# A decoder trunk on one core: embeddings loaded earlier and multiplied by eights, plain columns kept in banks, transposes by eights, longer runs of token-major pieces

## The chip, the cores and the metric

The kernel runs on one core of a Trainium2 chip. The metric is the device time of one execution in microseconds (us). TensorE (PE) multiplies, VectorE (DVE) and ScalarE (ACT) do elementwise work, GpSimd (POOL) and SyncE (SP) issue DMAs here. PE writes its products to PSUM, eight banks of 512 float32 columns on 128 partitions.

## The reference, cut to what matters

Two layers on 256 tokens of 2048 features: a gated linear-attention layer, then a forgetting-attention layer. Each ends with an MLP and a gated per-layer embedding, and these two are what the change touches:

```python
D_MODEL = 2048; SEQ = 256; DEPTH = 2; PLE_DIM = 256; D_FF = 4 * D_MODEL

def sq_relu_mlp(u, w_up, w_down):
    hid = jax.nn.relu(u @ w_up)
    return (hid * hid) @ w_down

for layer in range(DEPTH):
    u = rms_norm(h, mix_norm[layer])
    ...
    h = h + sq_relu_mlp(rms_norm(h, mlp_norm[layer]), w_mlp_up[layer], w_mlp_down[layer])
    gate = jax.nn.sigmoid(rms_norm(h, ple_norm[layer]) @ w_ple_gate[layer])
    h = h + (p[layer] @ w_ple_up[layer]) * gate
    ...
return rms_norm(h, final_norm)
```

All is float32. `p` is the embedding, 256 features for each token and layer.

## The kernel before

Activations lie feature-major: features on partitions, the 256 tokens along the row. Every float32 matrix is split into a rounded part `hi` and a rest `lo` (`split`, L105 to L111: ACT makes `whi` in L108, DVE makes `wlo` in L109), and a product is three matmuls: hi times hi, hi times lo, lo times hi. Weights come by the SP queue as tiles `raw` of 1 MB in three buffers; each tile is split in two halves of 1024 columns, for which there are four buffers `whi` and four `wlo`. What is normed by a row factor is multiplied first and scaled after (`rstd`).

A feature-major product (`mm_split`, L120 to L129) holds weights in PE and streams 256 tokens: 48 matmuls of 256 columns (L126 to L128) for one tile `ps` of 128 features. A token-major one (`product`, L292 to L299) holds activations and streams 512 weight columns: 12 matmuls for one piece.

The MLP (`mlp`, L239) goes through the 8192 hidden features in eight blocks of 1024. `up(b, i)` makes one tile of 128 hidden features: 48 matmuls, relu and scaling on DVE (L275), square on ACT (L277), split (`plain_split`, L219 and L220); for tiles 4 to 7 also four differences of it (L287), split in L289 and L290. The down product of a block is made while the next block's up tiles are made. Half of its columns go through seven products p1 to p7 on sums of quarters of the weights, in place of eight plain ones: the sums come into a buffer `chain` by DMAs that add, from the POOL queue (L258). The other half, the plain columns, goes through four pieces n0 to n3 of 24 matmuls. A finished product lies in a bank `pp` (four of them; the tiles `ps` have the other four) and is added to an accumulator in SBUF (`into`, L301 to L307). The order in which the pieces are written stands in a string of names in L390; the framework's scheduler may still move single instructions on an engine.

Behind the last block stands the last stage (L396 to L421): the accumulators are combined (L398); `h`, put away in DRAM at the start since `chain` has its place, is loaded again by POOL (L401); the eighth block's hidden tiles are multiplied feature-major, 24 matmuls for each of 16 tiles (L412 to L414), and with each tile go two transposes (L417) that bring the token-major sums back. Two adds to `h` follow (L418, L419), then the next layer's input is scaled and split (`u_p`) and its squares are summed (`ssq`).

Then the gate (`ple`, L424) opens a pool of its own, loads the embeddings by POOL (`praw`, L431), splits them to `pt` (L434), and for each of 16 tiles makes six matmuls of `pt`, which ACT copies to SBUF (L442), and 48 of `u_p`, scaled by `rstd`, put through a sigmoid (L449), multiplied and added to `h` (L453, L454). In layer 0 each column is then scaled and split twice for the next layer.

Of the kernel before, what the change touches and what calls it, by code (L numbers as in the profile page):

```python
# [10 lines left out]
F32 = mybir.dt.float32  # L11
# [7 lines left out]
P = 128  # L19
T = 256  # L20
D = 2048
KC = D // P
NBL = 8
NH = 16
# [10 lines left out]
def yoco_kernel(ctx, tc, a, out):  # L35
# [84 lines left out]
    def mm_split(pairs, act, kcs=KC, off=0):  # L120
        ps = psm.tile([P, T], F32, name="ps", tag="mm")
# [110 lines left out]
    def mlp(layer, u, stats, slots, u2, g2, pool, pps):  # L232
# [26 lines left out]
        acc = {}  # L259
        st2 = Stats()  # L260

        def up(b, i):
# [22 lines left out]
            x = pool.tile([P, 4, P], F32, name="sums", tag="sums", bufs=1)  # L285
# [23 lines left out]
        def bank():  # L309
            return pps.tile([P, 512], F32, name="pp", tag="pp", bufs=4)  # L310
# [11 lines left out]
        def down(b):  # L322
# [9 lines left out]
            got = {}  # L332
# [66 lines left out]
        sums = [(acc["2"], acc["4"]), (acc["3"], acc["7"]), (acc["n00"], acc["n01"]), (acc["n10"], acc["n11"])]  # L399
# [3 lines left out]
        last = a["w_down"][layer, 3 * KC :, :, 1024:].rearrange("n p f -> p n f")  # L403
        for n in range(KC):
# [4 lines left out]
            ps = psm.tile([P, T], F32, name="ps", tag="mm")  # L409
            for k in range(8):  # L410
                wh, wl = (w[:, k * P : (k + 1) * P] for w in pairs[n % 2])
                nc.tensor.matmul(ps, wh, nf[:, k, 0, :], start=k == 0, stop=False)  # L412
                nc.tensor.matmul(ps, wh, nf[:, k, 1, :], start=False, stop=False)  # L413
                nc.tensor.matmul(ps, wl, nf[:, k, 0, :], start=False, stop=k == 7)  # L414
# [560 lines left out]
```

## Time and profile before

| what | value |
|---|---|
| median of three runs | 2463.29 us (2462.58 to 2463.54) |
| the profiled execution, its span | 2462.49 us, 2460.8 us |
| PE, DVE, ACT, POOL busy in the span | 99%, 73%, 57%, 5% |
| granted TensorE clock, mean | 0.995 |
| matmuls recorded | 18024 |

The span is from the first to the last instruction; 1.7 us lie around it. Matmuls are pipelined, so one of 256 columns is recorded with 0.28 us although they start 0.11 apart; the distance between starts is what one costs in a run. The granted clock is 1.00 at 2.4 GHz and 0.50 at 1.2 GHz. Rows of the timeline have the start from the span's beginning, the duration, the engine, the line, out<-in, and in brackets how long the engine sat idle before and what ended it.

### The profile page before, as it was taken

The numbers are of one execution on the slowest core, as the hardware profiler recorded it, in microseconds if no ns is written. First come the engines' busy times: TensorE is split into PE (matmuls) and PEld (weight loads), VectorE is DVE, ScalarE is ACT, GpSimd is POOL, SyncE is SP. The second block draws the span as 40 slices with busy tenths as digits, with TensorE's granted clock in tenths as the row PEclk, the third lists the DMA queues.
The fourth block names the chain that finished last, engine by engine and source line by source line (L and its number), as shares of the span: only waits on it lengthen the run. The fifth ranks groups of instructions, "written<-read, shape, count | busy, mean of one in ns | idle before, by whom it ended". The sixth has DMA issues, their size and how long they took to land.

```text
span 2460.8 us, 43678 instructions
## 1 busy us (share of the span) xinstructions
PE 2437.6 (99%) x18024; PEld 2315.2 (94%) x18024; DVE 1801.9 (73%) x2802; ACT 1406.2 (57%) x2128; POOL 119.0 (5%) x159
## 2 busy tenths in 40 slices
PE   9999999999999999999999999999999999999998
PEld 8999999999999999999999999999999999999998
DVE  7897797676777777778774566667677777777866
ACT  7666575566555555555654545556655555555554
POOL 1000000000000000000000000000000000000000
PEclk9999999999999999999999999999999999999999
DMA  6455455578877887785555655557887888778653
GB/s 248 172 185 186 174 179 197 212 251 240 238 224 241 242 233 231 230 232 216 175 179 189 198 171 178 174 210 263 234 236 227 235 244 228 236 233 224 221 174 122
DMA packets 129271, 521.73 MB, mean 212 GB/s; under 512 B 8688, under 2 KB 9264, under 8 KB 91696
## 3 DMA queue, kind: packets, MB, share of 16 engines
q1 hardware_dynamic: 88256, 415.66, 47.4%
q0 software_dynamic: 39520, 101.25, 19.2%
q8 instruction: 141, 2.31, 0.4%
q10 hardware_dynamic: 1296, 2.03, 0.2%
q14 instruction: 58, 0.48, 0.1%
HBM read 512.58 MB, written 6.32 MB: 211 GB/s over the span
## 4 chain that ended last, share of the span: by engine, by line
PE 99%; DMA 0%; DVE 0%; ACT 0%; issue 0%; ACTq 0%; DVEq 0%; POOLq 0%
PE ps L126 21%; PE ps L127 21%; PE ps L128 21%; PE pp L297 8%; PE pp L299 8%; PE pp L298 8%; PE pst L146 2%; PE pst L145 2%; PE pst L147 2%; PE ps L412 1%; PE ps L414 1%; PE ps L413 1%; PE pa L635 0%; PE pl L837 0%; PE ptr L417 0%; DMA praw<-in_pT 0%
## 5 line engine op out<-in xcount | busy, mean ns | idle before, releaser
L109 DVE TENSOR_TENSOR wlo<-raw,whi 128x1024 fp32r<-128x1024 f32 (+2 forms) x798 | 965.7, 1211 | 420.8 <-ACT whi L108 411.4
L108 ACT CAST whi<-raw 128x1024 fp32r<-128x1024 f32 (+2 forms) x798 | 830.7, 1042 | 768.4 <-PE ps L127 585.4
L127 PE MATMUL ps<-u_m,whi 128*128 128x256 f32 x2048 | 565.2, 276 | 0.0
L126 PE MATMUL ps<-u_m,whi 128*128 128x256 f32 x2048 | 565.2, 276 | 0.0
L128 PE MATMUL ps<-u_m,wlo 128*128 128x256 f32 x2048 | 565.0, 276 | 0.0
L126 PEld LDWEIGHTS ps<-u_m,whi 128*128 128x128 f32 x2048 | 384.4, 188 | 4.3
L127 PEld LDWEIGHTS ps<-u_m,whi 128*128 128x128 f32 x2048 | 384.4, 188 | 4.3
L128 PEld LDWEIGHTS ps<-u_m,wlo 128*128 128x128 f32 x2048 | 384.6, 188 | 0.0
L298 PE MATMUL pp<-wlo,hid 128*128 128x512 f32 x840 | 327.3, 390 | 0.0
L299 PE MATMUL pp<-whi,hid 128*128 128x512 f32 x840 | 327.3, 390 | 0.0
L297 PE MATMUL pp<-whi,hid 128*128 128x512 f32 x840 | 318.6, 390 | 0.0
L108 ACT CAST whi<-chain 128x1024 fp32r<-128x1024 f32 x168 | 176.6, 1051 | 130.7 <-PE pp L299 78.0
L109 DVE TENSOR_TENSOR wlo<-chain,whi 128x1024 fp32r<-128x1024 f32 x168 | 204.7, 1223 | 51.7 <-ACT whi L108 48.6
L126 PE MATMUL ps<-u_a,whi 128*128 128x256 f32 x768 | 213.9, 279 | 0.0
L128 PE MATMUL ps<-u_a,wlo 128*128 128x256 f32 x768 | 213.2, 278 | 0.0
L127 PE MATMUL ps<-u_a,whi 128*128 128x256 f32 x768 | 212.3, 276 | 0.0
L299 PEld LDWEIGHTS pp<-whi,hid 128*128 128x128 f32 x840 | 157.7, 188 | 33.6
L298 PEld LDWEIGHTS pp<-wlo,hid 128*128 128x128 f32 x840 | 157.7, 188 | 29.1
L297 PEld LDWEIGHTS pp<-whi,hid 128*128 128x128 f32 x840 | 157.6, 188 | 29.0
L258 POOL DMA_DIRECT2D chain<-in_w_down x84 | 93.4, 1112 | 1104.9 <-DVE wlo L109 856.9
L126 PEld LDWEIGHTS ps<-u_a,whi 128*128 128x128 f32 x768 | 144.3, 188 | 0.3
L127 PEld LDWEIGHTS ps<-u_a,whi 128*128 128x128 f32 x768 | 144.3, 188 | 0.2
(289 smaller groups left out, 4704.1 us busy)
## 6 DMA issues: line engine op xcount, KB each, us to landing
raw<-in_w_up SPq DMA_DIRECT2D x128, 1024.0 KB, 6.1
raw<-in_w_down SPq DMA_DIRECT2D x86, 1024.0 KB, 5.2
chain<-in_w_down POOLq DMA_DIRECT2D x84, 1024.0 KB, 8.3
raw<-in_w_ain SPq DMA_DIRECT2D x48, 1024.0 KB, 4.8
raw<-in_w_pg SPq DMA_DIRECT2D x32, 1024.0 KB, 4.8
raw<-in_w_vf SPq DMA_DIRECT2D x20, 832.0 KB, 4.3
raw<-in_w_aout SPq DMA_DIRECT2D x16, 1024.0 KB, 4.8
raw<-in_w_k SPq DMA_DIRECT2D x16, 1024.0 KB, 4.7
```

Of the source, the lines that this page charges most:

```text
L108: nc.scalar.copy(h_, r)
L109: nc.vector.tensor_tensor(l_, r, h_.bitcast(F32), op=ALU.subtract)
L126: nc.tensor.matmul(ps, wk(pair, kl, 0), act[:, k, 0, :], start=st, stop=False)
L127: nc.tensor.matmul(ps, wk(pair, kl, 0), act[:, k, 1, :], start=False, stop=False)
L128: nc.tensor.matmul(ps, wk(pair, kl, 1), act[:, k, 0, :], start=False, stop=sp)
L145: nc.tensor.matmul(o, act[:, kk, 0, tok], hi, start=st, stop=False)
L146: nc.tensor.matmul(o, act[:, kk, 0, tok], lo, start=False, stop=False)
L147: nc.tensor.matmul(o, act[:, kk, 1, tok], hi, start=False, stop=sp)
L258: eng.dma_start(dst.rearrange("p (n f) -> p n f", n=4), src, **kw)
L297: nc.tensor.matmul(o, xh, hi, start=start and j == 0, stop=False)
L298: nc.tensor.matmul(o, xh, lo, start=False, stop=False)
L299: nc.tensor.matmul(o, xl, hi, start=False, stop=stop and j == 3)
```

## The change

Six things, in both layers:

- `embeddings` (L442 of the changed kernel on) loads `praw` and makes `pt` in the MLP's pool, called before the last stage. `praw` takes the place of the squares of the hidden tiles (`sqrs`), `pt` that of `scr`, in which relu results and sums lay.
- The gate multiplies `pt` by eights: before tiles 0 and 8, 48 matmuls for eight tiles go into four banks, two tiles to a bank, and ACT copies each bank in one go to accumulators that are free by then.
- The plain columns stay in four banks `pn00` to `pn11` over the seven blocks and are copied once, by ACT, to `nsum`. The products p1 to p7 share the four banks of the tiles `ps`.
- The transposes are made eight at a time (`back`), into two banks, and DVE adds two tiles of `h` at once.
- The string of the order has two up tiles in a row and then two to three token-major pieces.
- The gate lies inside the MLP's pools.

```diff
-    def mm_split(pairs, act, kcs=KC, off=0):
-        ps = psm.tile([P, T], F32, name="ps", tag="mm")
+    def mm_split(pairs, act, kcs=KC, off=0, ps=None):
+        if ps is None:
+            ps = psm.tile([P, T], F32, name="ps", tag="mm")
...
+        scr = pool.tile([P, 4 * T + 64], F32, name="scr", tag="scr", bufs=1)
+        squares = pool.tile([P, 3, T], F32, name="sqrs", tag="sqrs", bufs=1)
+        turn = [0, 0]
+
+        def part(which):
+            i = turn[which]
+            turn[which] = (i + 1) % (2 + which)
+            return squares[:, i, :] if which else scr[:, i * T : (i + 1) * T]
...
-            t = pool.tile([P, T], F32, name="up", tag="up", bufs=2)
+            t = part(0)
...
-            s = pool.tile([P, T], F32, name="hsq", tag="hsq", bufs=3)
+            s = part(1)
...
-        def bank():
-            return pps.tile([P, 512], F32, name="pp", tag="pp", bufs=4)
+        nbank = [[pps.tile([P, 512], F32, name=f"pn{c}{t}", tag=f"pn{c}{t}") for t in range(2)] for c in range(2)]
...
             def one(name, op, pairs):
-                o = bank()
+                o = psm.tile([P, 512], F32, name="pp", tag="mm")
...
-                if q == 0:
-                    got[c] = [bank() for _ in range(2)]
                 for t in range(2):
-                    product(got[c][t], lambda j: tuple(nf[:, 4 * q + j, w, t * P : (t + 1) * P] for w in range(2)), pairs, q == 0, q == 1)
-                if q == 1:
-                    for t in range(2):
-                        into(f"n{c}{t}", got[c][t])
+                    product(nbank[c][t], plain(q, t), pairs, b == q == 0, b == NBL - 2 and q == 1)
...
-            for item in "up p1 up p2 n0 up p5 up p3 n1 up p6 up n2 p7 up p4 up n3".split():
+            for item in "up up p1 p2 n0 up up p5 p3 n1 up up p6 n2 p7 up up p4 n3".split():
...
+        pt = embeddings(layer, pool)
...
+        nsum = pool.tile([P, 4, 512], F32, name="nsum", tag="nsum", bufs=1)
+        for i in range(4):
+            nc.scalar.copy(nsum[:, i], nbank[i // 2][i % 2])
...
+        def back(m):
+
+            for i in range(2):
+                n = 4 * m + 2 * i
+                ptr = pps.tile([P, 2, T], F32, name="ptr", tag=f"pn{m % 2}{i}")
+                for j in range(2):
+                    for t in range(2):
+                        nc.tensor.transpose(ptr[:, j, t * P : (t + 1) * P], sums[m][t][:, (n + j) % 4 * P : ((n + j) % 4 + 1) * P], ident)
+                nc.vector.tensor_tensor(h[:, n : n + 2, :], ptr, h[:, n : n + 2, :], op=ALU.add)
...
+            ps = mm_split([pairs[n % 2]], nf, 8)
+            if n % 4 == 0:
+                back(n // 4)
             nc.vector.tensor_tensor(h[:, n, :], ps, h[:, n, :], op=ALU.add)
-            nc.vector.tensor_tensor(h[:, n, :], pt, h[:, n, :], op=ALU.add)
...
+    def embeddings(layer, pool):
+        praw = pool.tile([P, 3, T], F32, name="praw", tag="sqrs", bufs=1)[:, :2, :]
+        pt = shifted(pool, 2, "pt", "scr", PTS)
         nc.gpsimd.dma_start(praw, a["pT"][layer])
         for k in range(2):
             plain_split(pt, k, praw[:, k, :])
+        return pt
...
-            pu = mm_split(wu, pt, kcs=2, off=2 * (n % 8))
-            up = pool.tile([P, T], F32, name="up", tag="up", bufs=2)
-            nc.scalar.copy(up, pu)
+                for i in range(4):
+                    pu = pps.tile([P, 2, T], F32, name="pu", tag=f"pn{i // 2}{i % 2}")
+                    for j in range(2):
+                        mm_split(wu, pt, 2, 4 * i + 2 * j, pu[:, j, :])
+                    nc.scalar.copy(ups[i], pu)
```

What this makes of the order on PE is shown at three places. The first is the end of the last stage of layer 0, before (`ptr` are the transposes, `accn` accumulators of the plain columns, `pt` the embeddings, `u_p` the gate's input):

```order
L412 MATMUL ps<-hid_7_11857,whi 128x256
L413 MATMUL ps<-hid_7_11857,whi 128x256
L414 MATMUL ps<-hid_7_11857,wlo 128x256
L417 MATMUL ptr<-ident,accn_7578 128x128
L417 MATMUL ptr<-ident,accn_7580 128x128
L126 MATMUL ps<-pt,whi 128x256
L126 MATMUL ps<-u_p_12733,whi 128x256
```

and now, on PE at the same place:

```order
L128 MATMUL ps<-hid_7_11671,whi 128x256
L129 MATMUL ps<-hid_7_11671,whi 128x256
L130 MATMUL ps<-hid_7_11671,wlo 128x256
L128 MATMUL pu<-pt,whi 128x256
L129 MATMUL pu<-pt,whi 128x256
L130 MATMUL pu<-pt,wlo 128x256
```

The transposes that stood behind the sixteenth tile have moved up to the thirteenth, and the embeddings' matmuls follow the tile's own; 48 of them stand there before the first of `u_p`.

The second place is PE in the middle of n0 of the first block now (`pn` are the banks of the plain columns, `ps` is the next up tile):

```order
L309 MATMUL pn_6164<-whi,hid_0_6168 128x512
L309 MATMUL pn_6165<-whi,hid_0_6168 128x512
L128 MATMUL ps<-u_m_5112,whi 128x256
L129 MATMUL ps<-u_m_5112,whi 128x256
L310 MATMUL pn_6164<-wlo,hid_0_6168 128x512
L311 MATMUL pn_6164<-whi,hid_0_6168 128x512
```

Two matmuls of the next up tile have moved in between the first two of n0's second half and the rest of it. It is so in n0 and in n1 of each of the 14 blocks, 28 times; before, a piece held none.

The third is the POOL queue around the reload of `h`, now (with the semaphores that each row waits for):

```order
L260 DMA chain<-in_w_down 128x4x512 [waits DMASW7_49,DVE_49]
L260 DMA chain<-in_w_down 128x4x512 [waits DMASW2_49,DVE_49]
L410 DMA h<-res 128x4096 [waits DMASW4_49,DMASW3_49,DVE_49]
L440 DMA praw<-in_pT 128x512 [waits DVE_49,PE_49,Pool_49]
L796 MEMSET cmask 128x128 [waits DVE_49,DMASW6_49,PE_49,Activation_49]
```

The DMAs stand in the order they had; what `praw` waits for on VectorE is now the split of the last hidden tile, and its wait for PE is for work of the attention before the MLP, where it was the last transpose of the stage.

## Rows read from the trace of the kernel before

**Rows 1.** The page: span, busy time of the engines, the granted clock of TensorE in 40 slices (tenths), and the chain that ended last by engine.

```profile
span 2460.8 us, 43678 instructions
PE 2437.6 (99%) x18024; PEld 2315.2 (94%) x18024; DVE 1801.9 (73%) x2802; ACT 1406.2 (57%) x2128; POOL 119.0 (5%) x159
...
PEclk9999999999999999999999999999999999999999
...
PE 99%; DMA 0%; DVE 0%; ACT 0%; issue 0%; ACTq 0%; DVEq 0%; POOLq 0%
```

**Rows 2.** The two largest of the waits of PE: who waited, for whom, us in total, times, the longest.

```profile
PE ps L126 <- ACT pt L219: 8.2, 2, 4.1
PE pst L145 <- ACT whi L108: 2.2, 1, 2.2
```

**Rows 3.** Timeline of all engines at the end of layer 0's MLP.

```profile
1168.76 0.38 PE L417 MATMUL ptr<-ident,accn 128*128 128x128 f32 x2
...
1169.71 0.57 POOL L431 DMA_DIRECT2D praw<-in_pT  x1 [64.11 <-DVE h L418]
...
1171.06 0.48 DVE L216 SCALAR_TENSOR_TENSOR u_p<-h,gains,u_p 128x256 fp32r<-128x256 f32 x1
...
1172.75 0.71 ACT L219 CAST pt<-praw 128x256 fp32r<-128x256 f32 x2 [1.99 <-DMA praw<-in_pT]
...
1173.21 0.58 PE L126 MATMUL ps<-pt,whi 128*128 128x256 f32 x1 [4.07 <-ACT pt L219]
```

**Rows 4.** DMA issues with the median time from issue to landing (line, queue, times, KB each, us), and from the timeline of POOL the issue of the reload.

```profile
h<-res POOLq DMA_DIRECT2D x2, 2048.0 KB, 8.5
...
praw<-in_pT POOLq DMA_DIRECT2D x2, 256.0 KB, 2.9
...
1105.04 0.57 POOL L401 DMA_DIRECT2D h<-res  x1 [21.00 <-DVE wlo L109]
```

**Rows 5.** Timeline of PE at the same place of layer 1.

```profile
2341.33 0.38 PE L417 MATMUL ptr<-ident,accn 128*128 128x128 f32 x2
2345.79 0.58 PE L126 MATMUL ps<-pt,whi 128*128 128x256 f32 x1 [4.08 <-ACT pt L219]
```

**Rows 6.** Stretches of PE: from:to and length in us, PE busy (matmuls that overlap the stretch), granted clock, DMA share, GB/s. In order: a long plain run; one block of the MLP; a run of 48 matmuls of 256 columns; one of 36 of 512; its last 30; what follows the gap of layer 0; the same of layer 1.

```profile
400.00:480.00 80.00, 80.00 (x708) 1.00 0.55 197
...
932.25:1017.05 84.80, 84.80 (x565) 1.00 0.81 236
1044.43:1049.91 5.48, 5.48 (x49) 1.00 1.09 287
1049.91:1058.09 8.18, 8.18 (x38) 1.00 0.87 287
1051.29:1058.09 6.80, 6.80 (x31) 1.00 0.85 290
...
1173.21:1176.49 3.28, 3.28 (x15) 0.50 0.73 287
...
2345.79:2350.68 4.89, 4.89 (x23) 0.50 0.51 188
```

**Rows 7.** Timeline of PE at four places: the start of an up tile, the first transpose of the layer, a pair of transposes in the last stage, three transposes in the attention.

```profile
1017.05 0.28 PE L126 MATMUL ps<-u_m,whi 128*128 128x256 f32 x1
...
1017.28 0.28 PE L128 MATMUL ps<-u_m,wlo 128*128 128x256 f32 x1
...
1110.31 0.27 PE L417 MATMUL ptr<-ident,acc 128*128 128x128 f32 x1
...
1126.71 0.38 PE L417 MATMUL ptr<-ident,acc 128*128 128x128 f32 x2
1126.85 0.36 PE L412 MATMUL ps<-hid,whi 128*128 128x256 f32 x1
...
1394.27 0.49 PE L860 MATMUL ptp<-ident,pe 128*128 128x128 f32 x3
1394.60 0.39 PE L836 MATMUL pl<-ksb,qsb 128*128 128x128 f32 x2
```

**Rows 8.** Timeline of VectorE: the two splits for the up tile that starts at 1017.05, and the first add to the reloaded `h`.

```profile
1014.25 2.59 DVE L109 TENSOR_TENSOR wlo<-raw,whi 128x1024 fp32r<-128x1024 f32 x2 [0.55 <-ACT whi L108]
...
1124.07 0.42 DVE L418 TENSOR_TENSOR h<-ps,h 128x256 f32<-128x256 f32 x1
```

**Rows 9.** Stretches of all engines, busy us and instructions of PE, PEld, DVE, ACT, POOL in this order, then granted clock, DMA share, GB/s: the last stage and the gate of layer 0.

```profile
1121.10:1168.90 47.80, 47.80 (x416) 47.79 (x414) 44.62 (x77) 29.19 (x47) 0.00 (x0) 1.00 0.53 186
1173.21:1273.43 100.22, 100.22 (x867) 100.14 (x867) 77.55 (x126) 63.75 (x114) 0.00 (x0) 0.98 0.52 179
```

**Rows 10.** Groups by line and shape: count, then busy us and mean ns of one, then idle time before them.

```profile
L109 DVE TENSOR_TENSOR wlo<-raw,whi 128x1024 fp32r<-128x1024 f32 x754 | 922.1, 1223 | 378.9 <-ACT whi L108 369.6
...
L275 DVE SCALAR_TENSOR_TENSOR up<-ps,rstd 128x256 f32<-128x256 f32 x128 | 54.3, 424 | 57.8 <-PE ps L128 57.7
L220 DVE TENSOR_TENSOR hid<-hsq,hid 128x256 fp32r<-128x256 f32 x128 | 53.6, 419 | 0.0
...
L290 DVE TENSOR_TENSOR hid<-sums,hid 128x512 fp32r<-128x512 f32 x56 | 38.5, 688 | 16.5 <-ACT hid L289 16.5
L307 DVE TENSOR_TENSOR accn<-accn,pp 128x512 f32<-128x512 f32 x48 | 32.6, 683 | 3.9 <-PE pp L299 3.9
L287 DVE TENSOR_TENSOR sums<-hsq,sums 128x128 f32<-128x128 f32 x112 | 32.0, 286 | 0.8
```

More of the change, by code (lines that the diff above doesn't have):

```diff
@@ L23 @@
 NBL = 8
+PTS = 28
 NH = 16
@@ L284, in up @@
             e = hid["first"]
-            x = pool.tile([P, 4, P], F32, name="sums", tag="sums", bufs=1)
+            x = scr[:, 2 * T : 4 * T].rearrange("p (f t) -> p f t", f=4)
             for i, (p, q) in enumerate(((e[:, P:], s[:, P:]), (e[:, :P], x[:, 0, :]), (e[:, P:], e[:, :P]), (s[:, :P], x[:, 1, :]))):
@@ L408, in mlp, with ple, two @@
                 pairs = [split(raw[:, i * 1024 : (i + 1) * 1024], 1024) for i in range(2)]
[L409 to L414, printed above, removed]
-            pt = pps.tile([P, T], F32, name="ptr", tag="pp", bufs=4)
-            for t in range(2):
-                nc.tensor.transpose(pt[:, t * P : (t + 1) * P], sums[n // 4][t][:, n % 4 * P : (n % 4 + 1) * P], ident)
+            ps = mm_split([pairs[n % 2]], nf, 8)
+            if n % 4 == 0:
+                back(n // 4)
             nc.vector.tensor_tensor(h[:, n, :], ps, h[:, n, :], op=ALU.add)
-            nc.vector.tensor_tensor(h[:, n, :], pt, h[:, n, :], op=ALU.add)
             scaled_split(u2(), n, g2)
             st2.add(n)
-        return st2
-    def ple(layer, u, stats, after):
-        with tc.tile_pool(name=f"pl{layer}", bufs=2) as pool:
-            ple_in(layer, u, stats, after, pool)
-    def ple_in(layer, u, stats, after, pool):
-        praw = pool.tile([P, 2, T], F32, name="praw", tag="praw", bufs=1)
+        return st2, pt
+    def embeddings(layer, pool):
+        praw = pool.tile([P, 3, T], F32, name="praw", tag="sqrs", bufs=1)[:, :2, :]
+        pt = shifted(pool, 2, "pt", "scr", PTS)
         nc.gpsimd.dma_start(praw, a["pT"][layer])
-        pt = shifted(pool, 2, "pt", "pt", 28)
         for k in range(2):
             plain_split(pt, k, praw[:, k, :])
+        return pt
+    def ple(layer, u, stats, pt, after, pool, pps):
+        def two(tag):
+            return pool.tile([P, 2, T], F32, name="ple" + tag, tag="acc" + tag, bufs=1)
+        gates, sigs = two("4"), two("7")
         rstd = None
-        wu = None
         for n in range(KC):
@@ L439, in ple_in @@
                 wu = load_slab(a["w_pu"][layer, n // 8], D, 2)
-            pu = mm_split(wu, pt, kcs=2, off=2 * (n % 8))
-            up = pool.tile([P, T], F32, name="up", tag="up", bufs=2)
-            nc.scalar.copy(up, pu)
+                if n == 0:
+                    ups = [two(i) for i in "1562"]
+                else:
+                    more = pool.tile([P, 4, 2, T], F32, name="ups", tag="nsum", bufs=1)
+                    ups = [more[:, i] for i in range(4)]
+                for i in range(4):
[3 more added lines that the diff above has]
+                    nc.scalar.copy(ups[i], pu)
+            up = ups[n % 8 // 2][:, n % 2, :]
             last = layer == 1 and n == KC - 1
@@ L445, in ple_in @@
             rstd = rstd or stats.rstd()
-            t = pool.tile([P, T], F32, name="gate", tag="gate", bufs=2)
+            t = gates[:, n % 2, :]
             nc.vector.tensor_tensor(t, ps, rstd, op=ALU.mult)
-            s = pool.tile([P, T], F32, name="sig", tag="sig", bufs=2)
+            s = sigs[:, n % 2, :]
             nc.scalar.activation(s, t, AF.Sigmoid)
@@ L755, in yoco_kernel, with after0 @@
     with tc.tile_pool(name="mp0", bufs=2) as mp, tc.tile_pool(name="mq0", bufs=1, space=PSUM) as mq:
-        stats = mlp(0, u_m, stats, "AB", up_, G_PLE + 0, mp, mq)
-    u_kv = slot("A", "u_kv")
-    u_q = slot("B", "u_q")
-    st_kv = Stats()
-    def after0(n):
-        scaled_split(u_kv, n, G_KV)
-        scaled_split(u_q, n, G_MIX + 1)
-        st_kv.add(n)
-    ple(0, up_(), stats, after0)
+        stats, pt = mlp(0, u_m, stats, "AB", up_, G_PLE + 0, mp, mq)
+        u_kv = slot("A", "u_kv")
+        u_q = slot("B", "u_q")
+        st_kv = Stats()
+        def after0(n):
+            scaled_split(u_kv, n, G_KV)
+            scaled_split(u_q, n, G_MIX + 1)
+            st_kv.add(n)
+        ple(0, up_(), stats, pt, after0, mp, mq)
     o_b = slot("C", "o_b")
```

16 lines of the change are left out of this document (8 added, 8 removed).

## The prediction

> **What bounds the kernel now.** I read the page first: TensorE (PE) is busy for 99% of the span and is the whole of the chain that ended last [rows 1]. So only what PE does, or waits for, counts. The waits of PE come second [rows 2]: the largest are two of 4.1 us for `pt`, the split embeddings, one in each layer, and the next is one of 2.2 us. There is none inside the MLP. Third, the timeline at such a wait: the last two transposes of the MLP start at 1168.76, the next matmul at 1173.21 [rows 3]. The reader is to see the whole chain there: the DMA of `praw` is issued at 1169.71, when `h L418` lets it go, since its buffer lies in a pool that opens once the MLP's pool is given back; it lands 2.9 us later [rows 4]; ScalarE casts at 1172.75, and PE starts. Layer 1 shows the same gap [rows 5]. Fourth, the granted clock by stretches: behind each gap PE runs at half rate (0.50, that is 1.2 GHz) for 3.28 and 4.89 us [rows 6]; in the stage before the gap it was 1.00 [rows 9]. Last, how PE spends busy time. In a long plain run a 256-column matmul starts every 80.00/706 = 0.1133 us (708 overlap the window, two at its edges), in the middle of a run a 512-column one every 6.80/30 = 0.2267 us [rows 6].
>
> **The change part by part**
>
> *Embeddings early.* `praw` and `pt` now take buffers of the MLP's own pool, free once the last hidden tile is split. On PE the stage ends with matmuls, and the embeddings' 48 follow directly. From the last pair of transposes to the first `pt` matmul go 4.45 and 4.46 us [rows 3, 5]; in the middle of the stage a pair takes 0.14 (1126.71 to 1126.85 [rows 7]). So 4.31 + 4.32 = **8.63 us** go, if nothing else is late. The half-rate stretches go with the gaps that came before them: half of 3.28 and of 4.89 is 1.64 + 2.45 = **4.09 us** [rows 6].
>
> What is late next? On POOL `praw` still stands behind the reload of `h`. In before the reload was issued at 1105.04, with 8.5 us to land [rows 4], and the first add to `h` stood at 1124.07 [rows 8]: 10.5 us to spare. Now the eighth up tile stands ahead of p4, so p4's split, which frees the buffer, comes one up tile (5.48 us) later: about 5 us stay. `praw` is issued some 3 us after the last up tile (an add of 0.68 and two splits of 1.22 stand ahead of its release on VectorE), and lands 2.9 us later, 8.5 if it has to wait for `h`; PE wants it after p4, n3 and the last stage, 2.74 + 5.46 + 47 us on. More than 40 us are spare. The casts of `pt` stand in ScalarE's queue, with casts of the next weights behind them; ScalarE is busy for 29.19 of 47.80 us there [rows 9], so 0.8 us of casts and a short wait for the DMA hide in that slack. If that cover were gone, a wait of 1 or 2 us in each layer would come back. At the start of the gate, PE wants the last column of `u_p` only after 48 + 45 matmuls, 10.5 us after the stage, and in before it was done at 1171.54, 2.8 us after the last transposes began [rows 3].
>
> *Longer runs.* A block of the MLP takes 84.80 us, and 384 matmuls of 256 and 180 of 512 columns at the plain rates make 43.52 + 40.80 = 84.32 [rows 6]. The 0.48 that is left falls on 8 changes to and fro: a run of 48 takes 5.48 where 5.44 are plain, one of 36 takes 8.18 where 8.16 are [rows 6], 0.04 + 0.02 = 0.06 for each pair. The new list has four pairs in a block in place of eight, 56 fewer in 14 blocks: 3.36 us. But the scheduler has put two matmuls of the next up tile into the middle of n0 and of n1, 28 times in all. No row of before has such a pair, so I bound it: at least nothing; at most a whole change, 28 x 0.06 = 1.68. I take what the rows show of its parts: two matmuls at the start of a run take 0.23 where 0.227 are plain [rows 7], and going back to 512 columns costs 0.02, so 0.024 each, 0.67 in all. **2.69 us** are left, between 1.68 and 3.36.
>
> *Transposes by eights.* The last stage takes 47.80 us [rows 9]: 384 plain matmuls are 43.52; 31 of a layer's 32 transposes (the first runs at 1110.3, within an up tile [rows 7]) at 0.11 each (three take 0.33 from 1394.27 to 1394.60 [rows 7]) are 3.41; 0.87 is left for 16 changes, 0.054 each. Now there are 4 groups in the stage: 12 x 0.054 = 0.65 in a layer, **1.30** in two. The count of transposes stays. If the 0.11 does not hold in longer groups (0.14 is what a pair took until the next start, and that is no full price), the term lies between 0.9 and 1.6.
>
> *Plain columns in banks.* It takes 48 adds of 0.683 us off VectorE [rows 10], none of them on the chain, and brings four ScalarE copies of a bank each at the end of each MLP, beside the last stage. Worth nothing by itself. It costs four banks for the whole MLP, so the other products now share four banks with the up tiles. A bank is wanted back four pieces later, 11 us at the least, and is read by an add of 0.68 or 0.42 us: free again in time unless VectorE is several us late.
>
> *Embeddings by eights.* Same matmuls, same shape, no change of shape around them: nothing on PE. Their splits no longer hold two of the four weight buffers through eight gate tiles, which can only help VectorE (busy for 77.55 of 100.22 us there [rows 9]).
>
> The sum is 8.63 + 4.09 + 2.69 + 1.30 = 16.7 us. Against the profiled execution (2462.49 us, 1.7 over its span) that is 2445.8. The median of the runs is 0.8 above that execution, so I forecast **2446.5 us**.
>
> **A rule that speaks against it.** Rows first: groups of three transposes [rows 7] and the pairs of the last stage ran at a granted clock of 1.00 [rows 9], and the stretches of 0.50 begin behind a gap of 4 us [rows 6]. The Trainium skill, "TensorE: Matmul & The Clock Gate", Part 4 (PE-mode transpose), says that transposes do not count as PE activity the way matmuls do, and that the full clock does not come on for them. The trace has no group of eight, so it cannot refute this for the new form; it makes it one of the rivals.
>
> **The rivals**
>
> 1. *The runs starve* (slower). VectorE has to deliver each weight half before PE wants it; the shortest lead I find in a run is 1.81 us (the split that starts at 1014.25 ends at 1015.47, its matmul starts at 1017.28 [rows 7, 8]). In a run of p, p, n (48 x 0.2267 = 10.88 us) it has 6 splits of 1.22, 2 adds of 0.68 and the tail of the second up tile (0.42 + 0.42 + 4 x 0.285 + 0.69 [rows 10]), 11.35 us in all, 0.47 more than PE takes. For it: that is over. Against it: in before the run p, n (8.18 us) has 4 splits, one add, that tail and every second time two more adds, 9.6 us, 1.4 over, and the lead held. It decides from the point where VectorE falls 1.81 us further behind than now. If it fell 2.4 us (two splits) behind, 42 long runs would wait 0.6 us each, 25 us: 2471 us. 5%.
> 2. *The gaps stay*, since `pt` or something ahead of it in a queue is late: only 2.69 + 1.30 are left, 2459.3 us, within 0.2% of before. Against it are the 40 us to spare. 3%.
> 3. *A short wait takes the gap's place*, at the weights of the embeddings, the copies of the plain columns or the adds to `h`: 2 us in each layer, without a fall of the clock: 2450.5 us. The 5 us left for `h` are the tightest place. 7%.
> 4. *Eight transposes in a row let the clock fall.* If each of the eight groups brought a half-rate stretch as a gap does now, 8 x 1.64 to 8 x 2.45 = 13 to 20 us would come back: 2460 to 2466 us. Against it: a group is 0.9 us long and the gaps were 4. 3%.
>
> **How the numbers follow.** The forecast has 82%, from 2444.5 (short insertions free, other terms at their ends) to 2448.5. The range is wider: down to 2442.5 for terms that are 2 us too small in sum, and up to 2455, which takes in rival 3 with a wait of up to 4 us in each layer. What a measurement of this kernel can tell from no change is about 0.2%, 4.9 us, so the border lies at 2458.4. Faster: 82 + 7% = 89%; within: rival 2 and half of rival 4, 5%; slower: rival 1 and the other half, 6%.
>
> **What would show it.** Right: no wait of PE for `pt`; a granted clock of 1.00 from the first microseconds to the tail; a block of the MLP at about 84.6 us instead of 84.80; the last stage at about 47.1 instead of 47.80. Wrong: a wait of PE at the second half of a token-major piece, for `wlo` (rival 1); PE waiting for a copy of the embeddings' products or at the first gate tile (rival 3); a stretch of 0.50 behind a group of transposes (rival 4). A block above 84.7 us would show that the short insertions cost more than I take.

## The result and the profile after

| | before | after |
|---|---|---|
| median of four runs each, taken together (us) | 2463.41 (2462.58 to 2463.55) | 2446.57 (2446.45 to 2447.05) |
| profiled execution (us) | 2462.49 | 2446.62 |
| span of it (us) | 2460.8 | 2444.9 |
| mean granted clock | 0.995 | 0.997 |

The ratio of the times is 0.9933, with a 95% interval of 0.9915 to 0.995: faster by 16.8 us, where 16.7 were forecast (2446.5 us). The total is right; one of its terms isn't, and a later section tells which. One execution of e2 (3037.58 us, granted clock 0.751) and one of e3 (4105.46 us, 0.555, the one that was profiled) ran far slower than the others of the same kernel and are left out of the medians below, so no trace of e3 is used.

From the profile's page after: the span, the busy time of each engine with its share and its instructions, and the chain that ended last by engine:

```profile
span 2444.9 us, 43569 instructions
PE 2429.5 (99%) x18024; PEld 2307.3 (94%) x18024; DVE 1761.3 (72%) x2738; ACT 1409.9 (58%) x2112; POOL 119.2 (5%) x159
PE 99%; DVE 0%; ACT 0%; DMA 0%; issue 0%; ACTq 0%; DVEq 0%
```

Against [rows 1]: TensorE is busy for 8.1 us less, and the span is 15.9 us shorter; the rest is time in which it was idle. VectorE has 64 instructions and 41 us less, which nothing waited for. The chain is still all TensorE, so each microsecond of the difference has to be found on that engine.

All waits of TensorE after (engine, line, what it waited for; sum in us, times, longest):

```profile
PE pst L147 <- ACT whi L109: 2.4, 1, 2.4
PE ps_ssqc L190 <- DVE sq L165: 2.0, 1, 2.0
PE ps_spread L199 <- DVE diag L198: 1.1, 1, 1.1
PE warm L64 <- POOL ones L60: 1.1, 1, 1.1
```

The two waits of 4.1 us for `pt` [rows 2] are gone and none has come in their place. Where the embeddings are now, in layer 0 (line, operation, count, duration in ns as min/median/max, first and last start in us):

```profile
L440 POOL DMA_DIRECT2D praw<-in_pT x1: 570/570/570, 1117.4 to 1117.4; - x1
L222 DVE TENSOR_TENSOR pt<-praw,pt x2: 418/422/425, 1123.6 to 1124.0; 128x256 fp32r<-128x256 f32 x2
L128 PE MATMUL pu<-pt,whi x16: 275/275/275, 1167.2 to 1172.3; 128*128 128x256 f32 x16
```

`pt` is whole at 1124.4, TensorE wants it at 1167.2: 43 us to spare, where the prediction had counted more than 40. The tighter transfer was the reload of `h`:

```profile
1109.24 0.57 POOL L410 DMA_DIRECT2D h<-res  x1 [20.81 <-DVE wlo L110]
1124.31 1.28 DVE L422 TENSOR_TENSOR h<-ptr,h 128x512 f32<-128x512 f32 x2
```

It is issued at 1109.24, takes 8.2 us to land by the DMA view, and the first add comes at 1124.31: about 7 us to spare (5 in the prediction).

TensorE by stretches (start and end, length; busy time and instructions of PE, weight loads, VectorE, ScalarE, POOL; granted clock, DMA share, GB/s): a block of the MLP, the last stage of the MLP in layers 0 and 1, the 48 products with the embeddings, the gate stage up to the next layer's first matmul, and the gate stage of layer 1 up to TensorE's end:

```profile
931.41:1016.11 84.70, 84.70 (x565) 77.50 (x564) 61.55 (x82) 47.44 (x58) 6.67 (x6) 1.00 0.80 237
1120.17:1167.19 47.02, 47.02 (x415) 47.02 (x414) 41.63 (x72) 29.05 (x49) 0.00 (x0) 1.00 0.55 195
2285.31:2332.34 47.03, 47.03 (x416) 47.03 (x415) 41.65 (x72) 29.07 (x49) 0.00 (x0) 1.00 0.56 192
1167.19:1172.63 5.44, 5.44 (x50) 5.44 (x49) 3.93 (x7) 4.30 (x7) 0.00 (x0) 1.00 0.67 227
1167.19:1265.62 98.43, 98.43 (x868) 98.38 (x867) 79.11 (x130) 66.39 (x108) 0.00 (x0) 1.00 0.55 190
2332.34:2436.18 103.84, 100.73 (x880) 100.25 (x878) 68.43 (x105) 61.25 (x96) 0.00 (x0) 0.99 0.43 148
```

and the same two gate stages in the kernel before:

```profile
1168.90:1273.43 104.53, 100.46 (x870) 100.15 (x868) 80.37 (x131) 66.00 (x118) 0.57 (x1) 0.98 0.52 177
2341.47:2452.05 110.58, 103.42 (x881) 102.70 (x879) 69.52 (x107) 60.81 (x106) 0.57 (x1) 0.96 0.41 137
```

So the difference is made up like this:

- the gate stages: 104.53 - 98.43 = 6.10 and 110.58 - 103.84 = 6.74, together 12.84 us (forecast 8.63 + 4.09 = 12.72);
- the blocks of the MLP: 84.80 [rows 6] against 84.70, fourteen times: 1.4 us (forecast 2.69);
- the last stages: 47.80 [rows 9] against 47.02, twice: 1.55 us. From this go the transposes that the scheduler put ahead of the stage. After, there is a pair in each layer, in a run of 48 matmuls of 512 columns, which takes 11.15 us with it (1089.92 to 1101.07) where the others take 10.90: 0.25 us. Before, it was a single one, in an up tile, and cost 0.1. So 0.15 us a layer is given back, and 1.25 us are left (forecast 1.30).

That is 15.5 of the 15.9 us between the spans. The other 0.4 lies in the part ahead of the MLP's first 512-column matmul: it starts at 537.89 after and at 532.89 before, where one up tile (5.44 us) less stands ahead of it. The change doesn't touch this part, and it differs between executions: in after's own profile and those of six kernels below that are the same up to there, TensorE starts that matmul between 537.74 and 538.95 us. So a difference of about a microsecond between two medians is read from the traces of the stretches here, not from the medians alone.

Why do the blocks save only half? The timeline of one of the 28 places where the scheduler put two matmuls of the next up tile into n0 or n1 (start, duration with the pipeline's latency, engine and line, operation):

```profile
969.61 0.39 PE L311 MATMUL pn<-whi,hid 128*128 128x512 f32 x1
969.83 0.39 PE L309 MATMUL pn<-whi,hid 128*128 128x512 f32 x1
970.06 0.28 PE L128 MATMUL ps<-u_m,whi 128*128 128x256 f32 x1
970.17 0.28 PE L129 MATMUL ps<-u_m,whi 128*128 128x256 f32 x1
970.29 0.40 PE L310 MATMUL pn<-wlo,hid 128*128 128x512 f32 x1
970.52 0.40 PE L311 MATMUL pn<-whi,hid 128*128 128x512 f32 x1
970.76 0.40 PE L309 MATMUL pn<-whi,hid 128*128 128x512 f32 x1
```

The two take 0.23 us, as forecast. But read the starts behind them, and the stretch to the end of the run:

```profile
970.29:972.63 2.34, 2.34 (x13) 1.89 (x12) 1.47 (x3) 1.05 (x1) 0.00 (x0) 1.00 1.08 370
```

Ten matmuls of 512 columns lie in it (the counts take in three that overlap its edges): 0.234 us each, at a granted clock of 1.00, where the plain rate (the distance between starts in the middle of a long run) is 0.2267 [rows 6]. That is 0.07 us in each of the 28 places, 2 us in the kernel.

### The profile page after: what moved, and what is told of

It is laid out like the page before. It is cut to its first block, busy times and chain, and to the rows that moved or that the text cites. A ratio compares the mean times of both kernels' runs of the same rounds, so it can differ in the third digit from the quotient of the medians.

```text
span 2444.9 us, 43569 instructions
## 1 busy us (share of the span) xinstructions
PE 2429.5 (99%) x18024; PEld 2307.3 (94%) x18024; DVE 1761.3 (72%) x2738; ACT 1409.9 (58%) x2112; POOL 119.2 (5%) x159
## 4 chain that ended last, share of the span: by engine, by line
PE 99%; DVE 0%; ACT 0%; DMA 0%; issue 0%; ACTq 0%; DVEq 0%
PE ps L128 21%; PE ps L130 21%; PE ps L129 21%; PE pn L311 4%; PE pn L310 4%; PE pn L309 4%; PE pp L309 4%; PE pp L311 4%; PE pp L310 4%; PE pst L147 2%; PE pst L148 2%; PE pst L149 2%; PE pu L130 0%; PE pu L128 0%; PE pu L129 0%; PE pa L658 0%
## 5 line engine op out<-in xcount | busy, mean ns | idle before, releaser
L311 PE MATMUL pn<-whi,hid 128*128 128x512 f32 x448 | 175.1, 391 | 0.0
L310 PE MATMUL pn<-wlo,hid 128*128 128x512 f32 x448 | 175.1, 391 | 0.0
L309 PE MATMUL pn<-whi,hid 128*128 128x512 f32 x448 | 160.5, 390 | 0.0
L309 PE MATMUL pp<-whi,hid 128*128 128x512 f32 x392 | 152.9, 390 | 0.0
L310 PE MATMUL pp<-wlo,hid 128*128 128x512 f32 x392 | 152.8, 390 | 0.0
L311 PE MATMUL pp<-whi,hid 128*128 128x512 f32 x392 | 152.8, 390 | 0.0
```

The source lines that it names most:

```text
L309: nc.tensor.matmul(o, xh, hi, start=start and j == 0, stop=False)
L310: nc.tensor.matmul(o, xh, lo, start=False, stop=False)
L311: nc.tensor.matmul(o, xl, hi, start=False, stop=stop and j == 3)
```

## The experiments

The theory after the result: the gap and the half rate behind it are one thing and are gone because `pt` is there in time; changes of shape cost 0.06 us a pair as forecast; the short insertions cost 0.07 and not 0.024; banks and VectorE's adds cost nothing. The rivals are in the expectations. Times are medians of up to eleven runs; after is 2446.57 us throughout, and before was measured again beside each group (2463.32, 2463.27 and 2462.58 us). After was not, so a difference of about a microsecond from it rests on the traces.

**e1: the embeddings alone** (against before; the call stands ahead of the last stage, and the products stay six by six)

```diff
+        pt = embeddings(layer, pool)
...
-        praw = pool.tile([P, 2, T], F32, name="praw", tag="praw", bufs=1)
+        praw = pool.tile([P, 3, T], F32, name="praw", tag="sqrs", bufs=1)[:, :2, :]
-        pt = shifted(pool, 2, "pt", "pt", 28)
+        pt = shifted(pool, 2, "pt", "scr", PTS)
```

> The kernel before with one part of the change alone: the embeddings are loaded and split ahead of the last stage of the MLP, in buffers of the MLP's pool; the products with them stay six by six in each gate tile, the order of the run string, the plain columns and the transposes two by two stay as before. Theory (the gap and the half rate behind it have one cause, the late embeddings): both go, 8.63 + 4.09 = 12.72 us less than before, 2450.7 us, with no TensorE wait for pt and the granted clock 1.00 in the gate stage. Rival A (the clock falls for another reason): only the gaps go, 2454.8 us, and some 8 us at 0.50 stay. Rival B (a wait for another operand takes the gap's place): 2459 to 2463 us.

Measured: 2449.21 us (2448.51 to 2449.36), ratio to before 0.9944 (0.9932 to 0.9956), 14.1 us less. No wait for `pt` is left. The gate stage from the last transposes on, in layer 0 and, from 2335.00, in layer 1:

```profile
1168.15:1174.43 6.28, 6.28 (x57) 6.28 (x56) 4.03 (x6) 3.13 (x5) 0.00 (x0) 1.00 0.54 189
1174.43:1266.89 92.46, 92.46 (x814) 92.38 (x813) 75.65 (x123) 62.18 (x111) 0.00 (x0) 1.00 0.55 184
2335.00:2438.91 103.91, 100.83 (x880) 100.34 (x878) 68.79 (x104) 59.93 (x104) 0.00 (x0) 0.99 0.42 144
```

From the last transpose's start to the next layer's first matmul it is 98.77 us here and 104.56 in before; from layer 1's to TensorE's end 104.01 and 110.61: together 12.4 us, the forecast's 12.7 within 0.3. The other 1.7 us of the medians lie in untouched code or in the scatter. This one part is most of the change, and rivals A and B fall.

**e2: the embeddings late again** (against after)

```diff
-        pt = embeddings(layer, pool)
...
-        return st2, pt
+        return st2, embeddings(layer, pool)
...
-        praw = pool.tile([P, 3, T], F32, name="praw", tag="sqrs", bufs=1)[:, :2, :]
+        praw = pool.tile([P, 4, 512], F32, name="praw", tag="nsum", bufs=1)[:, 0, :].rearrange("p (k t) -> p k t", k=2)
...
+        nc.vector.tensor_copy(praw[:, 0, 0:1], h[:, KC - 1, 0:1])
         nc.gpsimd.dma_start(praw, a["pT"][layer])
```

> The kernel after, with the embeddings put late again: their load writes a buffer that a VectorE copy of the last column of h has just read out, so it can't start before the last add of the MLP. In the order of TensorE's instructions the 48 products with the embeddings now stand behind the 48 of the first gate tile (5.44 us), where they stood in front of them. Theory (what costs is only that something waits for pt with nothing else queued ahead of it): 5.44 us of gate matmuls cover most of the 4.45 us from the last transposes of before to its first product with pt, so the time is 2446.6 to 2449 us, at 1.00. Rival (the early load itself is what saves): the gaps and the half rate come back, 2446.6 + 12.7 = 2459.3 us.

The copy writes into the buffer of the load and reads the last column of `h`, so the load has to wait for the last add. Measured: 2446.04 us, as after. Its embeddings in layer 0, and the gate stage from its first matmul on:

```profile
L439 POOL DMA_DIRECT2D praw<-in_pT x1: 570/570/570, 1169.8 to 1169.8; - x1
L222 DVE TENSOR_TENSOR pt<-praw,pt x2: 418/419/420, 1173.3 to 1173.7; 128x256 fp32r<-128x256 f32 x2
L128 PE MATMUL pu<-pt,whi x16: 275/275/287, 1174.4 to 1180.8; 128*128 128x256 f32 x16
1168.25:1266.68 98.43, 98.43 (x868) 98.38 (x867) 80.31 (x133) 66.71 (x110) 0.57 (x1) 1.00 0.56 192
```

The load starts 1.5 us behind the first gate matmul (1168.25), `pt` is whole at 1174.1, the first product starts at 1174.4, and TensorE has waited for nothing: the stage takes 98.43 us, the same as after to the hundredth. So the early load is enough (e1), but it isn't needed. What cost 12.7 us in before was the late load together with the order: the 48 matmuls of the first gate tile, which here run while `pt` is made, stood behind the products with `pt` on TensorE.

**e3: the old order of the blocks** (against after)

```diff
-"up up p1 p2 n0 up up p5 p3 n1 up up p6 n2 p7 up up p4 n3"
+"up p1 up p2 n0 up p5 up p3 n1 up p6 up n2 p7 up p4 up n3"
```

> The kernel after with the string that sets the order in a block of the MLP put back to that of before (up one at a time, 8 pieces of the plain columns, token-major pieces between). Theory (the runs as measured: the 14 blocks take 84.70 us against 84.80): 14 x 0.10 = 1.4 us slower than after, 2448.0 us, a block of 84.80. Rival A (the longer runs save what was forecast): 2.7 us slower, 2449.3 us. Rival B (longer runs starve TensorE somewhere): faster than after.

Measured: 2448.13 us, 1.6 us slower than after: nearer to the theory's 1.4 than to the forecast's 2.7. By itself a median doesn't settle a difference of one microsecond; the blocks of e4 and e5 below do, by their parts.

**e4 and e12: the pieces in another order, no short insertion** (against after)

```diff
-"up up p1 p2 n0 up up p5 p3 n1 up up p6 n2 p7 up up p4 n3"
+"up up p1 n0 p2 up up p5 n1 p3 up up p6 n2 p7 up up p4 n3"
```

> The kernel after with one piece of the plain columns moved in each half of a block (p1 n0 p2 and p5 n1 p3 in place of p1 p2 n0 and p5 p3 n1), which leaves no insertion of only two 256-column matmuls within a run of 512-column ones. Theory (each of the 28 short insertions costs about 0.07 us: two switches, and the ten matmuls behind it start 234 ns apart where others start 227): 28 x 0.07 = 2.0 us faster than after, 2444.6 us, a block of 84.56. Rival A (an insertion costs the 0.024 us of the forecast): 0.7 us faster, 2445.9 us. Rival B (the time is from something else in the block, and the order of the pieces is indifferent): 2446.6 us.

> e4_pnp once more, for the comparison with e11_four_up_again: 1.6 us less than after by the blocks of its trace, 2445.0 us, or the 2443.7 us of its first run if the blocks aren't all.

Measured: 2443.69 us, and 2445.22 in its second run. A block:

```profile
930.92:1015.48 84.56, 84.56 (x565) 77.48 (x564) 61.85 (x82) 47.44 (x58) 6.67 (x6) 1.00 0.82 237
```

84.70 has become 84.56 with two insertions fewer: 0.07 us each, the theory's price, three times the forecast's. Over the two layers the traces give 1.6 us and not 2.0: in the last block of each layer the scheduler now puts single transposes into the runs, and 34 matmuls behind one of them run at 0.233. The two medians (2.9 and 1.4 us below after) lie on both sides of that.

**e9: insertions of several lengths** (against e4)

```diff
+IDLE = (1, 2, 3, 4, 6, 12, 24)
...
+                if idle and j == 2:
+                    io = psm.tile([P, T], F32, name="idle", tag="mm")
+                    for i in range(idle):
+                        nc.tensor.matmul(io, xh, hi[:, :T], start=i == 0, stop=i == idle - 1)
```

> e4_pnp with idle 256-column matmuls (sums not used) put into one run of 48 matmuls of 512 columns in each of the seven blocks of a layer, in its middle, with 24 behind them: 1, 2, 3, 4, 6, 12 and 24 of them in blocks 1 to 7. It measures the cost of an insertion by itself. Theory A (behind any short insertion the rest of the run stays at 234 ns a matmul, however short or long it is, up to some number): behind one to six the 24 take 5.61 us, behind 24 idle ones 5.46 (three at 234, then 227). Theory B (only behind two, as seen in after, the state stays; it is a matter of odd or even): behind 1 and 3 otherwise than behind 2 and 4. Theory C (the state comes from breaking off a sum in its bank, not from the insertion): all seven alike, 5.61 us also behind 24.

Measured: 2458.2 us in one execution. The 24 matmuls of 512 columns behind 1, 6, 12 and 24 idle ones of 256, in layer 0 (the columns as above):

```profile
565.13:570.73 5.60, 5.60 (x27) 4.54 (x25) 3.32 (x5) 3.16 (x3) 1.27 (x1) 1.00 0.96 243
905.83:911.43 5.60, 5.60 (x26) 4.54 (x25) 3.32 (x5) 3.17 (x4) 1.27 (x1) 1.00 0.79 186
991.98:997.58 5.60, 5.60 (x27) 4.54 (x25) 2.99 (x4) 2.46 (x3) 0.84 (x1) 1.00 0.93 184
1079.54:1084.98 5.44, 5.44 (x27) 4.51 (x25) 1.23 (x2) 3.07 (x4) 0.00 (x0) 1.00 1.08 186
```

5.60 / 24 = 0.233 us each behind 1, 2, 3, 4, 6 and 12, and 5.44 / 24 = 0.2267 behind 24; layer 1 shows the same seven values. Theory A holds for insertions of 256 columns, with its turn between 12 and 24 (behind 24 even the first three are at the plain rate, so 5.44 and not its 5.46). Odd or even (B) makes no difference, and since the sum is broken off in its bank in all seven (C), that isn't the cause either. An insertion is paid for by all that is left of the run behind it: 24 x 0.0067 = 0.16 us here, 10 x 0.007 = 0.07 in after.

**e5 and e11: two runs of four up tiles; e10: one run of eight** (against after; the first new line is that of e5 and e11, the second that of e10)

```diff
-"up up p1 p2 n0 up up p5 p3 n1 up up p6 n2 p7 up up p4 n3"
+"up up up up p1 n0 p2 p5 n1 p3 up up up up p6 n2 p7 n3 p4"
+"up up up up up up up up p1 n0 p2 p5 n1 p3 p6 n2 p7 n3 p4"
```

> The kernel after with the up tiles of a block in two runs of four (up up up up p1 n0 p2 p5 n1 p3 up up up up p6 n2 p7 n3 p4), so TensorE changes between 256 and 512 columns 30 times in place of e4_pnp's 58, with no insertion of two. Theory (each pair of changes costs 0.06 us, as 84.80 us with eight pairs in a block and e4_pnp's 84.56 with four say, and nothing starves): 28 x 0.06 = 1.7 us less than e4_pnp, some 2442.0 us, a block of 84.44. Rival (the starving of the prediction's first rival: a run of four up tiles is 21.8 us of TensorE in which VectorE has to keep up with four tiles' splits, twice as long as in after): waits for wlo or nf in the blocks, 2446 us or more.

> e5_four_up once more, beside e4_pnp in the same call, since their traces differ by 1.2 us and their first medians do not. Theory (the traces' blocks decide; the first medians hold 1 us of difference in the unchanged front part): 0.7 to 1.7 us less than e12_pnp_again. Rival (something outside the blocks gives it back): equal medians again.

> The kernel after with all eight up tiles of a block in one run of 43.6 us, then all its token-major pieces: 14 pairs of changes fewer than e5_four_up. Theory (pairs cost 0.06 us each and nothing starves): a block of 84.38 in place of 84.44, 0.8 us less than e5_four_up. Rival (the first rival of the prediction: VectorE and ScalarE fall behind in so long a run): waits for whi, wlo or a bank in the runs, a block over 84.5, 2446 us or more.

Measured: e5 2443.9 us and e11 2443.61 (ratio to before 0.9924, 0.9912 to 0.9937); e10 2511.11 (1.0195, 1.0181 to 1.0209). A block of e5:

```profile
908.50:992.93 84.43, 84.43 (x565) 77.38 (x564) 61.52 (x83) 47.65 (x58) 6.67 (x6) 1.00 0.80 237
```

Two pairs of changes fewer than e4 and 0.12 to 0.13 us less: 0.06 a pair, for the second time. Yet e5's median missed its theory: it lies 0.2 us above e4's first, not 1.7 below. Measured together with e12, e11 is 1.6 us faster (expected 0.7 to 1.7). By the traces the step from e4 is 1.2 us in the MLPs and not 1.7: behind the single transpose in the last block of each layer now stand 70 matmuls at 0.234 us (16.40 us from 1102.52 in e5) where e4 has 34. TensorE waits for nothing in these blocks, so the first rival of the prediction does not begin at runs of 21.8 us. But its traces show the next thing to be late. ScalarE's waits for the weights that come by way of `chain`, first in e5 (after has no such row), then in e10, followed by the waits of TensorE there:

```profile
ACT whi L109 <- DMA chain<-in_w_down: 22.5, 13, 2.4
```

```profile
ACT whi L109 <- DMA chain<-in_w_down: 150.9, 45, 9.1
PE pp L309 <- ACT whi L109: 24.0, 14, 3.5
PE pp L310 <- DVE wlo L110: 9.3, 14, 0.8
POOL chain L260 <- DVE wlo L110: 589.5, 68, 44.4
```

At runs of four this wait is hidden; with all pieces in one run it reaches TensorE. One place in e10 (start, duration, engine, line, operation, in brackets the idle time before it and what ended it), and two stretches behind it:

```profile
592.17 0.39 PE L311 MATMUL pp<-whi,hid 128*128 128x512 f32 x1
592.78 1.99 ACT L109 CAST whi<-chain 128x1024 fp32r<-128x1024 f32 x2 [6.58 <-DMA chain<-in_w_down]
593.88 0.50 PE L309 MATMUL pp<-whi,hid 128*128 128x512 f32 x1 [1.31 <-ACT whi L109]
595.13 0.50 PE L310 MATMUL pp<-wlo,hid 128*128 128x512 f32 x1 [0.76 <-DVE wlo L110]
```

```profile
596.20:599.60 3.40, 3.40 (x10) 2.63 (x9) 2.33 (x4) 2.00 (x3) 1.26 (x1) 0.51 0.71 107
599.83:616.16 16.33, 16.33 (x72) 13.22 (x70) 9.51 (x9) 9.17 (x10) 1.55 (x2) 1.00 0.90 282
```

ScalarE stands idle for 6.58 us until the `chain` transfer lands, TensorE then waits 1.31 and 0.76 us, the granted clock is down at its lower level (0.51 over 3.4 us), and then the 70 matmuls that are left of the run go at 16.33 / 70 = 0.233 us. Blocks of e10 take 87.6 to 90.9 us.

The half rate follows in 12 of the 14 places. Here is one of the other two, with the stretch behind it:

```profile
861.76 0.50 PE L309 MATMUL pp<-whi,hid 128*128 128x512 f32 x1 [1.37 <-ACT whi L109]
863.02 0.50 PE L310 MATMUL pp<-wlo,hid 128*128 128x512 f32 x1 [0.76 <-DVE wlo L110]
863.35:882.48 19.13, 19.13 (x83) 15.49 (x82) 14.40 (x15) 10.35 (x11) 2.81 (x3) 1.00 0.89 254
```

The waits are as long as in the place above, the clock stays at 1.00, and the 82 matmuls behind them still go at 0.233 us. So the length of the waits alone doesn't decide on the half rate, and the slower spacing doesn't need it. In 3 of the 14 places the run goes back to 0.2267 us behind the half rate.

**e6: TensorE kept busy in the gap** (against before)

```diff
+IDLE = 36
...
+        idle = psm.tile([P, T], F32, name="idle", tag="mm")
+        for j in range(IDLE):
+            nc.tensor.matmul(idle, u[:, j % 14, 0, :P], u[:, j % 14, 0, :], start=j == 0, stop=j == IDLE - 1)
```

> The kernel before with 36 idle matmuls of 256 columns (4.08 us, their sums are not used) on TensorE between the last transposes of the MLP and the first product with pt, in both layers, so that TensorE isn't idle while the embeddings come. Theory (the half rate behind the gap comes from TensorE's idle time): the products with pt start as late as before, but the granted clock stays 1.00 behind them, so 4.09 us less than before, 2459.3 us. Rival A (the half rate has another cause, at this place in the program): as before, 2463.4 us. Rival B (the idle matmuls hold up the first product): 2463 us or more, with a later start of pt.

Measured: 2458.67 us, ratio to before 0.9982 (0.9973 to 0.9991), 4.6 us less. The stretches of both layers, from the idle matmuls on:

```profile
1165.00:1173.50 8.50, 8.50 (x75) 8.50 (x75) 6.86 (x14) 4.36 (x8) 0.57 (x1) 1.00 0.59 182
1173.50:1180.00 6.50, 6.50 (x58) 6.47 (x57) 1.81 (x3) 1.81 (x4) 0.00 (x0) 1.00 0.32 129
2344.00:2352.00 8.00, 8.00 (x69) 7.86 (x68) 2.05 (x4) 3.28 (x6) 0.00 (x0) 1.00 0.28 115
```

The first product with `pt` comes 4.48 and 4.52 us after the last transposes, as late as in before, and the clock stays at 1.00 (2.4 GHz). The 54 matmuls that follow take 6.20 and 6.25 us where before they took 7.80 and 8.57: 3.9 us. So the half rate does come from TensorE's idle time, and 4.09 was its price within 0.2. Both rivals fall.

**e7: transposes two at a time** (against after)

```diff
-            for i in range(2):
-                n = 4 * m + 2 * i
-                ptr = pps.tile([P, 2, T], F32, name="ptr", tag=f"pn{m % 2}{i}")
...
+            ptr = pps.tile([P, 2, T], F32, name="ptr", tag=f"pn{m // 2 % 2}{m % 2}")
+            for t in range(2):
+                nc.tensor.transpose(ptr[:, 0, t * P : (t + 1) * P], sums[m // 4][t][:, m % 4 * P : (m % 4 + 1) * P], ident)
...
-            if n % 4 == 0:
-                back(n // 4)
+            back(n)
```

> The kernel after with the transposes of the last stage of the MLP two at a time again (one bank each, one add each), behind each tile of 24 matmuls. Theory (the groups of eight save 0.62 us a layer as read from the traces): 1.2 us slower than after, 2447.8 us, a last stage of 47.8 us in place of 47.02. Rival A (groups of eight let the clock fall or hold up the adds somewhere, as the fourth rival of the prediction has it): equal or faster than after. Rival B (two banks more in use at a time make TensorE wait for an add): a wait of the transposes, over 2449 us.

Measured: 2447.75 us, 1.2 slower than after, as expected. The last stage, up to the first product with `pt`, takes 47.69 us where after takes 47.02:

```profile
1120.53:1168.22 47.69, 47.69 (x416) 47.69 (x414) 41.44 (x77) 28.93 (x48) 0.00 (x0) 1.00 0.55 190
```

With the gate stage, which here follows a pair of transposes, it is 146.24 us up to the next layer's first matmul (1266.77) against 145.45: 0.8 a layer by the trace, 1.6 in two. TensorE waits for no add, so rival B falls; it is slower than after, so A falls too. Another 0.2 us lies in layer 0's last block: behind the early pair of transposes the 34 matmuls of 512 columns stay at 0.233 us (8.02 us from 1093.41). Behind the same pair in layer 1, and in both layers of after (7.82 us from 1093.25), they come back to 0.2267.

**e8: the plain columns out of their banks in every block** (against after; the new function copies a bank in the first block and adds it in the others)

```diff
-                    product(nbank[c][t], plain(q, t), pairs, b == q == 0, b == NBL - 2 and q == 1)
+                    product(nbank[c][t], plain(q, t), pairs, q == 0, q == 1)
+                    if q == 1:
+                        keep(c, t, b)
```

> The kernel after with the sums of the plain columns taken out of their banks in every block, by ScalarE in the first and by VectorE adds of 128x512 (688 ns each, 24 a layer) in the others, as before. Theory (these adds lie beside TensorE, which waits for none of them): as after, 2446.6 us within 0.3, VectorE's busy time 33 us more. Rival (VectorE is late in the longer runs, so the banks were needed to make them possible): waits of TensorE in the blocks, 2448 us or more.

Measured: 2446.43 us (2446.05 to 2446.7), as after, with 48 more instructions and 28 us more on VectorE:

```profile
PE 2429.8 (99%) x18024; PEld 2307.4 (94%) x18024; DVE 1789.4 (73%) x2786; ACT 1410.0 (58%) x2112; POOL 119.7 (5%) x159
```

No wait of TensorE, all full blocks at 84.71 us. Banks for the plain columns buy nothing at this length of the runs.

## Why the prediction was right, and where it was not

- *Embeddings early, 8.63 + 4.09 us.* Right in path and size: 12.84 us in the gate stages of after, 12.4 with this part alone (e1), and 3.9 for the clock alone (e6). What I had not seen is that a load as late as in e2 costs nothing either once gate matmuls stand ahead of the products. The prediction took the lateness for the cause; the cause is the lateness together with TensorE's order.
- *Longer runs, 2.69 us.* This is the term that was mis-sized: 1.4 us, under the lower end of its own range (1.68). Its first half held: a pair of changes costs 0.06 us, by the steps from 84.70 to 84.56 (insertions out) and to 84.44 (pairs out), and from 84.80 to 84.56 for four pairs. The step that failed is the 0.024 us for a short insertion. I took "going back to 512 columns costs 0.02" from a run of 36 behind 48 matmuls of 256 columns [rows 6], where only the first three matmuls behind the change are slow (235, 233 and 232 ns, then 227); behind two matmuls all ten that are left are slow, and the insertion costs 0.073. That is above even the upper bound, a whole pair at 0.06: a bound from the nearest rows held only for the rows' own length of run. The prediction's own sign for this, a block above 84.7, came only at its border: 84.70 to 84.71 where about 84.6 was expected.
- *Transposes by eights, 1.30 us.* Right: 1.25 us by the trace of after, 1.6 by that of e7 and 1.2 by its median; the prediction's range is 0.9 to 1.6. The early pair, which gives back 0.15 us a layer, stood in no term.
- *Plain columns in banks, embeddings by eights, 0.* Right for the banks (e8). The products by eights were not undone by themselves; they take 5.44 us for 48, the plain rate. The 866 matmuls of the gate stage behind a pair of transposes take 98.74 and 98.60 us in the two layers of e1, where the products stand six by six, and 98.55 and 98.56 in e7, where they stand by eights: at most 0.2 us a layer.
- *Rival 1, the runs starve.* Not in after, nor in runs twice as long (e5). It does exist: e10 is 65 us slower than after. Its place is not the one I had named (VectorE too slow for the splits) but one step earlier: the `chain` transfers, which are issued only when VectorE has split what lay in their buffer (the POOL row of e10).
- *Rivals 2 and 3.* No wait for `pt`, at the weights or the adds; the reload of `h` had 7 us to spare.
- *Rival 4.* The groups of eight take 0.79 us each (the first has six left in the stage) and the granted clock is 1.00 over both last stages. The Trainium skill, "TensorE: Matmul & The Clock Gate", Part 4 (PE-mode transpose), says that transposes don't count as activity as matmuls do; at this length, with 96 matmuls between the groups, the trace shows no effect of it. Longer groups weren't tried.
- The total came within 0.1 us of the median, and that is partly luck. By the traces the terms made 15.5 us and not 16.7, since 1.3 us of the longer runs are missing. About as much came from elsewhere: 0.4 us from the part ahead of the MLP, and 0.9 because the medians differ by 16.8 us where the two profiled spans differ by 15.9.

The best version found is e5's order (2443.6 to 2443.9 us), 2.8 us below after by the traces of its two MLPs and as much by its medians.

## What to carry to other kernels

Where an engine that takes its instructions in order waits for one late operand, look first for ready work that can stand in front of it: here 48 matmuls ahead of the wait were worth as much as the early load, and the granted clock stayed at 1.00 with them. When a scheduler slips a few instructions of another shape into a long run, price what is behind them in the run (here 0.0067 us for each 512-column matmul), not the few themselves, and check by the starts of successive matmuls. Lengthen runs only as far as the operands' own transfers keep up: here two runs of four gained, one run of eight lost 65 us.

## What the hardware showed that was not expected

- The spacing of 512-column matmuls has two values at one granted clock of 1.00: 226.7 ns and 233 to 234 ns. After 24 or more matmuls of 256 columns it is back at the lower one at once or from the fourth on; behind 1 to 12 it stays at the higher to the end of the run (e9). It also stays there behind a single transpose (e4, 34 matmuls; e5, 70) and behind waits, with or without a stretch at half rate (e10, 70 and 82 matmuls).
- The length of what interrupts the run doesn't decide this alone. Behind the same pair of transposes the 34 matmuls came back from the fourth on in both layers of after and in layer 1 of e7, and stayed at the higher value in layer 0 of e7; behind the waits of e10, 3 of 14 runs came back. What in the engine holds this state, no run shows.
- In e10 the half rate follows two waits of TensorE close behind one another, as short as 1.26 and 0.76 us, where the gap of before was over 4 us. It follows in 12 of 14 such places: waits of 1.37 and 0.76 us and of 1.51 and 0.77 left the clock at 1.00. What decides, no run shows.
